# A streaming encoder layer: pool weights folded into the output projection, norm roots by DRAM, more column groups, slots of a multiple of 256 bytes, and products of two contraction blocks in turn

## The chip, the cores and the metric

The kernel runs on 1 core of one Trainium2 chip. The metric is the device time of the program in microseconds, the median of several runs. TensorE (PE in the profile) does matrix products, VectorE is DVE, ScalarE is ACT, GpSimd is POOL; SyncE (SP) issues most DMAs. PSUM has eight banks of 128 x 512 float32, SBUF holds the tiles.

## The reference

One layer of a hybrid encoder, applied to 2048 prompt frames and to 32 frames of a running stream (the sample), with model width 1024. Everything is float32.

```python
def layer(x, pool_hist, n_valid, S0, ...):
    h = rmsnorm(x, g_pre_mix)
    z = h @ w_in                                  # 1024 x 2560: u, q, f, i, g of 512 columns each
    u, zq, zf, zi, zg = jnp.split(z, [...], axis=-1)
    u_ext = concat([pool_hist, u], axis=1)
    y_pool = pool_mix(u_ext, n_valid, w_pool, pool_scale)
    ...                                           # q, gate f, key, log f from zq, zf
    S1, o = hgrn_run(S0, q, kin, zi, logf)        # gated recurrence, 4 heads x 128
    y_hg = rmsnorm(o, g_hg_norm) * silu(zg)
    y_mix = concat([y_pool, y_hg], axis=-1) @ w_out
    x = x + rmsnorm(y_mix, g_post_mix)
    h2 = rmsnorm(x, g_pre_ffn)
    f = (silu(h2 @ w_gate) * (h2 @ w_up)) @ w_down   # 1024 x 2816 and back
    x = x + rmsnorm(f, g_post_ffn)
    return x, u_ext[:, -15:], S1

def pool_mix(u_ext, n_valid, w_pool, pool_scale):
    for g, w in enumerate((2, 4, 8, 16)):         # 4 groups of 128 channels
        d_g = (trailing sum of w frames) / min(t + 1 + n_valid, w) - u_g
    y = einsum('blgc,gcd->blgd', d, w_pool)       # one 128 x 128 map for each group
    return y * pool_scale
```

## The kernel before

**Precision.** Every large product is made of three TensorE products in float32r: each operand is split into a high part (ScalarE copies it to float32r) and a low part (VectorE subtracts), and high x high, high x low and low x high are summed in a PSUM bank. A product of 128 x 128 stationary and 128 x 512 moving elements is the unit; the program has 8,232 of them. Small work (pool maps, the recurrence's blocks, transposes, the sample's frames) is done in plain float32, where one product is two passes in the trace.

**Stages.** The prompt is worked in two halves of 1024 frames, A (`S.B` False) and B (`S.B` True), B with the 32 sample frames. For each half, in TensorE's order: the values (`first_values` or `values`: the i columns, frames stationary), four heads (`head_products`: columns f, q and g, weights stationary, activations `hT` moving, in banks `mmb`), four pool groups 3, 2, 1, 0 (`pool_products`), the output projection (`project`, banks `ops`), then gate and up (`gate_up`, banks `gx`, `gy`, `gz`, `gw`, with seven products in place of eight for each pair of blocks). At the end `down` makes the second feed-forward product for all frames (banks `dx`, `dy`, `dz`).

**What runs between.** The recurrence of a head (`hgrn`), the pool windows, norms and statistics are written as generators. A `Task` holds one; `poll()`, called after every three products, advances those whose time has come on a clock `Pace.t` that adds an assumed time for each TensorE instruction. So TensorE's order is fixed when the program is written; the orders of the other engines and of SP's DMAs come from the framework's scheduler. `finish()` makes all that is left of a task. `take()`, `ahead()` and `raws()` load and split weight blocks some steps ahead of their use.

**The recurrence's blocks.** `group` makes 32 x 16 or 32 x 32 blocks of scores for each 32 frames, with the output in the PSUM partitions 32j to 32j+31 of the bank `gb`: four column groups. The level-5 blocks go to partitions 0 and 64 (two column groups), the 64 x 64 blocks `lv` to partitions 0 to 63 (one).

**The pool stage.** `pool_window` makes the windowed means on VectorE directly behind a group's products. `pool_mix`, a task, multiplies by `w_pool` on TensorE (bank `pps`, full float32, 128 x 512, two for a group and half), scales and splits the result into `S.y[g]`, and in B transposes the last 15 frames of each group out (`nps`).

**The norm at B's start.** `later_stats` sums the squares of B's frames while A runs. `front_norm` spreads the roots over the partitions: POOL makes diagonal matrices `dg`, and TensorE multiplies them by ones (bank `rb`). The sample's frames are scaled and transposed by TensorE (`stps`). `late_constants` loads `w_pool` and transposes the pool cache (`cps`).

**Memory.** Tiles live in slots: 39 of `TMAX` = 1056 float32 (4,224 bytes, 16.5 times 256), and `NT` = 22 of 512 float32 (2,048 bytes). Slots stand one behind the other, so every second slot of the first kind starts 128 bytes past a multiple of 256.

Of the kernel before, what the change touches and what calls it, by code (L numbers as in the profile page):

```python
# [29 lines left out]
NT = 22  # L30
# [4 lines left out]
TMAX = HALF + NS  # L35
CHUNK = 128
# [41 lines left out]
def body(tc, ins, outs, cst):  # L78
    nc = tc.nc
    ctx = ExitStack()  # L80
    with ctx:
# [7 lines left out]

        def ztile(name, shape=None, dt=F32):  # L90
            return UP.tile(shape or [P, TMAX], dt, tag="u", name=name)

        def xtile(name, shape=None):
            return UP.tile(shape or [P, TMAX], F32R, tag="u", name=name)

# [45 lines left out]
        wpool = CP.tile([P, 4, P], F32, name="wpool")  # L141
        hist = CP.tile([P, 4, 16], F32, name="hist")
        shist = CP.tile([P, 4, 16], F32, name="shist")
# [9 lines left out]
        def late_constants():  # L153
            nc.sync.dma_start(out=wpool, in_=ins["w_pool"][0].rearrange("g c d -> c g d"))
            cachet = ztile("cachet", [HIST, 512])
            nc.sync.dma_start(out=cachet, in_=ins["cache_pool"][0, 0])
            cps = axbank("cps")
            for g in range(4):
                nc.tensor.transpose(cps[:, 16 * g:16 * g + HIST], cachet[:, g * P:(g + 1) * P], ident[0:HIST, 0:HIST])
            nc.vector.tensor_copy(shist[:, :, 0:HIST], cps[:, 0:64].rearrange("p (g t) -> p g t", g=4)[:, :, 0:HIST])  # L160
# [113 lines left out]

        def gemm_cols(w, act, n0, n1, ps):
            _, hi, lo = w
            n = n1 - n0
            cnt = 3 * len(act)
            i = 0
            for k, (ah, al) in enumerate(act):  # L280
                wh, wl = (x[k // 4][:, (k % 4) * P:(k % 4 + 1) * P] for x in (hi, lo))
                for a, b in ((wh, ah), (wh, al), (wl, ah)):
                    mm(ps[:, 0:n], a, b[:, n0:n1], i == 0, i == cnt - 1, rcost(n))
                    i += 1
                poll()
# [151 lines left out]
        def later_stats(S):  # L437

            st = S.st
            for i in range(NCH):  # L440
# [6 lines left out]
                yield 20000.0  # L447
            ev = st[:, 0:16].rearrange("p (i c) -> p i c", c=2)
# [3 lines left out]
            S.rs = [[st[:, 24 + 4 * tg + i:25 + 4 * tg + i] for i in range(4)] for tg in range(2)]  # L452

        def scaled_channels(S, tg):
            rb = axbank("rb")
            for i in range(4):
                mm(rb[:, i * P:(i + 1) * P], ones, S.dg[tg][:, i], True, True, 112.0)
# [17 lines left out]
        def front_norm(S, tg):  # L475
            if tg == 0:
                S.hsr = SP.tile([P, KD, NS], F32, tag="hs", name="hsr", bufs=1)
                S.ysr = SP.tile([P, KD, NS], F32, tag="ysr", name="ysr", bufs=1)
            channel_tiles(S, tg)
            S.dg[tg] = t2("dg", [P, 4, P])  # L480
            for i in range(4):
                nc.gpsimd.tensor_scalar(S.dg[tg][:, i], ident, S.rs[tg][i], None, ALU.mult)
            if tg == 1:
                xq = ztile("xts", [NS, D])
                nc.sync.dma_start(out=xq, in_=x_s)
# [3 lines left out]
            if tg == 1:  # L489
                st = new_stat()  # L490
                sumsq(xq, NS, st[0:NS, 0:1])
                nc.vector.tensor_scalar(xq, xq, rstd_of(st, NS), None, ALU.mult)
            yield from scaled_channels(S, tg)
            if tg == 1:
                sample_to_channels(xq, g_pre, S.hsr)


        def front_loads(S):
# [111 lines left out]
        def values(S, tg):  # L610
# [4 lines left out]
            for k in range(0, KD, 2):  # L615
# [5 lines left out]
                for kk in range(2):  # L621
                    ah, al = S.hT[k + kk]
                    for i in range(4):
                        value_products(pss, i, ah, al, (tg * 4 + i) * P, hi[kk], lo[kk], k + kk == 0, k + kk == KD - 1)
                        poll()
# [1080 lines left out]
```

## Time and profile before

| | |
|---|---|
| median of 3 runs | 2145.66 us (2145.22 to 2146.64) |
| the profiled execution | 2145.8 us, of which the span is 2144.0 |
| granted TensorE clock | 0.998 of full speed |
| TensorE | 99% busy, 13,176 passes |
| VectorE, ScalarE, GpSimd | 67%, 38%, 13% busy |
| DMA | 316.19 MB moved, 147 GB/s on average |

A span is the time from the first to the last instruction. A row of the profile names a line, an engine, an operation, and the tile written and the tiles read. TensorE's line is nearly always L180, the helper `mm`, so rows are told apart by their tiles. A product's length in the trace, some 0.39 us, has its drain in it; what counts is the time from one product's start to the next's. "x434" counts instructions, and idle time stands behind a bar with what ended it.

### The profile page before, as it was taken

The page shows a single profiled execution, that of the slowest core. Times are in us where ns is not written, and L with a number is a line of the kernel's source. Part 1 is how long each engine was busy: PE and PEld are TensorE (multiplying, and loading weights), DVE is VectorE, ACT ScalarE, POOL GpSimd, SP SyncE. Part 2 cuts the span into 40 slices and gives each one's busy share as a digit, 9 for nine tenths or more (in the row PEclk, how much of TensorE's full clock was granted, in tenths as well). Part 3 has the DMA queues.
Part 4 walks back from the last instruction along what each step waited for, and adds up shares of the span by engine and source line. Part 5 has one row for each costly group of instructions (what it writes and reads, how often), then busy time and mean ns, then how long its engine had stood idle before and what let it go on. Part 6 is the DMA issues. An engine that isn't in the chain of part 4 may idle for free.

```text
span 2144.0 us, 34134 instructions
## 1 busy us (share of the span) xinstructions
PE 2124.1 (99%) x13176; PEld 1702.8 (79%) x13176; DVE 1431.6 (67%) x2330; ACT 822.0 (38%) x1605; POOL 281.6 (13%) x382
## 2 busy tenths in 40 slices
PE   9999999999999999999999999999999999999998
PEld 8788778888888887788867778888888777877876
DVE  6655665787776778355574697767667756466487
ACT  6434335544444445233323664444444521011032
POOL 1223301100000010122320220000000211110134
PEclk9999999999999999999999999999999999999999
DMA  8121134445545559011004624544445796776778
GB/s 305 50 70 56 35 128 157 128 123 167 157 144 156 148 162 286 27 44 34 25 23 149 189 85 131 156 143 143 144 143 145 234 323 197 224 222 189 223 214 217
DMA packets 388783, 316.19 MB, mean 147 GB/s; under 512 B 16007, under 2 KB 318335, under 8 KB 388622
## 3 DMA queue, kind: packets, MB, share of 16 engines
q1 hardware_dynamic: 386174, 306.11, 46.5%
q0 software_dynamic: 2016, 7.34, 1.8%
q8 instruction: 104, 1.70, 0.3%
q14 instruction: 57, 0.47, 0.1%
q10 hardware_dynamic: 432, 0.57, 0.1%
HBM read 215.60 MB, written 98.37 MB: 146 GB/s over the span
## 4 chain that ended last, share of the span: by engine, by line
PE 82%; DVE 4%; ACT 1%; issue 1%; POOL 1%; DMA 1%; DVEq 0%; POOLq 0%; SPq 0%; ACTq 0%
PE gx L180 21%; PE gy L180 11%; PE dx L180 10%; PE mmb L180 10%; PE ops L180 9%; PE dy L180 5%; PE gz L180 4%; PE dz L180 3%; PE vps L180 2%; PE gw L180 1%; PE gsps L180 1%; PE gb L180 1%; DVE acc L1493 1%; PE ups L180 1%; PE pps L180 1%
## 5 line engine op out<-in xcount | busy, mean ns | idle before, releaser
L180 PE MATMUL gx<-fhi,wf 128*128 128x512 f32 x1376 | 449.1, 395 | 0.0
L180 PEld LDWEIGHTS gx<-fhi,wf 128*128 128x128 f32 x1376 | 258.3, 188 | 61.4 <-issue 2.2
L180 PE MATMUL gx<-flo,wf 128*128 128x512 f32 x688 | 270.0, 392 | 0.0
L180 PE MATMUL gy<-fhi,wf 128*128 128x512 f32 x704 | 233.0, 393 | 0.1
L180 PE MATMUL mmb<-hThi,whi 128*128 128x512 f32 x512 | 217.6, 425 | 0.0
L180 PE MATMUL dx<-dhi,hst 128*128 128x512 f32 x640 | 213.4, 394 | 0.5 <-DVE acc L1493 0.4
L180 PE MATMUL mmb<-hThi,wlo 128*128 128x512 f32 x512 | 201.7, 394 | 0.0
L180 PE MATMUL mmb<-hTlo,whi 128*128 128x512 f32 x512 | 201.5, 394 | 0.0
L1493 DVE TENSOR_TENSOR acc<-dx,acc 128x512 f32<-128x512 f32 x168 | 115.2, 689 | 75.9 <-PE dx L180 75.2
L1217 DVE TENSOR_TENSOR wf<-s,wf 128x512 fp32r<-128x512 f32 x176 | 120.1, 689 | 62.2 <-ACT wf L1212 59.6
L180 PEld LDWEIGHTS gy<-fhi,wf 128*128 128x128 f32 x704 | 132.2, 188 | 31.2 <-DVE c L1315 0.5
L180 PEld LDWEIGHTS gx<-flo,wf 128*128 128x128 f32 x688 | 129.4, 188 | 28.3
L1212 ACT CAST wf<-s 128x512 fp32r<-128x512 f32 x176 | 108.3, 621 | 101.0 <-PE gy L180 30.3
L180 PEld LDWEIGHTS dx<-dhi,hst 128*128 128x128 f32 x640 | 120.1, 188 | 32.2 <-issue 3.4
L180 PE MATMUL gy<-flo,wf 128*128 128x512 f32 x352 | 138.2, 393 | 0.0
L180 PE MATMUL dx<-dlo,hst 128*128 128x512 f32 x320 | 125.5, 392 | 0.0
L1217 DVE TENSOR_TENSOR wf<-wraw,wf 128x512 fp32r<-128x512 f32 x132 | 89.8, 688 | 44.2 <-ACT wf L1212 44.1
L180 PEld LDWEIGHTS mmb<-hThi,whi 128*128 128x128 f32 x512 | 96.6, 189 | 24.4 <-issue 5.4
L180 PEld LDWEIGHTS mmb<-hThi,wlo 128*128 128x128 f32 x512 | 96.4, 188 | 22.3
L180 PE MATMUL dy<-dhi,hst 128*128 128x512 f32 x320 | 112.9, 393 | 1.0 <-DVE acc L1493 1.0
L1212 ACT CAST wf<-wraw 128x512 fp32r<-128x512 f32 x132 | 80.9, 621 | 83.5 <-PE gx L180 38.3
L180 PEld LDWEIGHTS mmb<-hTlo,whi 128*128 128x128 f32 x512 | 96.8, 189 | 18.7 <-issue 2.4
(332 smaller groups left out, 4093.2 us busy)
## 6 DMA issues: line engine op xcount, KB each, us to landing
hst<-hdFalse SPq DMA_DIRECT2D x140, 256.0 KB, 3.0
hst<-hdTrue SPq DMA_DIRECT2D x140, 256.0 KB, 3.1
wraw<-in_w_gate_dram SPq DMA_DIRECT2D x50, 512.0 KB, 4.2
wraw<-in_w_up_dram SPq DMA_DIRECT2D x50, 512.0 KB, 4.1
hdFalse<-hhi SPq DMA_DIRECT2D x77, 256.0 KB, 2.3
hdFalse<-hlo SPq DMA_DIRECT2D x77, 256.0 KB, 2.4
hdTrue<-hhi SPq DMA_DIRECT2D x77, 256.0 KB, 2.6
hdTrue<-hlo SPq DMA_DIRECT2D x77, 256.0 KB, 2.6
```

What stands on the lines that cost most here:

```text
L180: nc.tensor.matmul(out, l, r, start=start, stop=stop, skip_group_check=more)
L1212: nc.scalar.copy(wf[:, 0], getattr(M, src) if isinstance(src, str) else src)
L1217: nc.vector.tensor_tensor(wf[:, 1], getattr(M, src) if isinstance(src, str) else src, wf[:, 0].bitcast(F32), ALU.subtract)
L1493: nc.vector.tensor_tensor(dst, ps, dst, ALU.add)
```

## The change

1. **Slots.** `SLOT` = 1024 + 64 float32 (4,352 bytes, 17 times 256) takes the place of 1056; `NT` is 21. `wpool` and `shist` are gone from the constants.

```diff
-NT = 22
+NT = 21
+SLOT = HALF + 64
-            return UP.tile(shape or [P, TMAX], dt, tag="u", name=name)
+            return UP.tile(shape or [P, SLOT], dt, tag="u", name=name)
```

2. **Products in turn.** `in_turn` takes the three products of two contraction blocks alternately, so that no product has an operand of the one before it. It is used in `gemm_cols`, `values`, `project`, and the `product` of `gate_up` and `down` (where the group has one pair, the three are only put into another order). `first_values` keeps its order.

```diff
+        def in_turn(trios):
+            for a, b in ((0, 2), (0, 3), (1, 2)) if len(trios) > 1 else ((0, 2), (1, 2), (0, 3)):
+                for t in trios:
+                    yield t[a], t[b]
...
-                for kk in range(4):
-                    bh, bl = (x[:, (kk % 2) * 512:(kk % 2) * 512 + 512] for x in F[kk // 2])
-                    wh, wl = wf[:, 0, kk * P:(kk + 1) * P], wf[:, 1, kk * P:(kk + 1) * P]
-                    for n, (a, b) in enumerate(((wh, bh), (wh, bl), (wl, bh))):
-                        mm(ps, a, b, start and kk == 0 and n == 0, kk == 3 and n == 2, rcost(512), not start)
-                    poll()
+                for k in (0, 2):
+                    trios = [(*(wf[:, i, kk * P:(kk + 1) * P] for i in range(2)),
+                              *(x[:, (kk % 2) * 512:(kk % 2) * 512 + 512] for x in F[kk // 2])) for kk in (k, k + 1)]
+                    for n, (a, b) in enumerate(in_turn(trios)):
+                        mm(ps, a, b, start and k == 0 and n == 0, k == 2 and n == 5, rcost(512), not start)
+                        if n % 3 == 2:
+                            poll()
```

3. **Pool weights folded.** A task in half A makes `mixed` = w_pool x scale x the first 512 rows of w_out, writes it to DRAM, and the projections load those rows from there. The windowed mean goes to the projection without a map between; `pool_mix` and its products are gone. The windows are a task now, with VectorE's steps 1300 ns apart.

```diff
+        def mixed_weights():
+            wt = t2("wpt", [P, 4, P])
+            nc.sync.dma_start(out=wt, in_=ins["w_pool_t"].rearrange("g d c -> d g c"))
...
+            load(*todo[0])
+            yield 6000.0
             for g in range(4):
+                nc.scalar.activation(wt[:, g], wt[:, g], AF.Copy, scale=p_scale[:, g:g + 1])
+            for n, (g, dh) in enumerate(todo):
+                if n + 1 < len(todo):
+                    load(*todo[n + 1])
+                ps = axbank("wmp")
+                mm(ps, wt[:, g], rows.pop((g, dh)), True, True, 858.0)
+                out = t2("wmo")
+                nc.scalar.copy(out, ps)
+                nc.sync.dma_start(out=mixed[g * P:(g + 1) * P, dh * 512:dh * 512 + 512], in_=out)
+                yield 4000.0
...
-                        want(lambda ki=ki, dh=dh: raw_rows2(w_out, KORDER[ki], dh * 512))
+                        want(lambda ki=ki, dh=dh: raw_rows2(mixed if KORDER[ki] < 4 else w_out, KORDER[ki], dh * 512))
...
-                ps = axbank("pps")
-                mm(ps, wpool[:, g, :], d_t[:, sbk * 512:(sbk + 1) * 512], True, True, 858.0)
...
+            put_y(S, g, slice(0, HALF), d)
```

4. **Roots by DRAM, inputs in channels.** `later_stats` also sums the sample's squares and writes the 1,056 roots to DRAM; B's `front_norm` loads them broadcast over the partitions in place of `dg` and `rb`. The sample's frames and the pool cache come transposed as inputs, so `stps` of the first norm and `cps` are gone. The eight `nps` transposes are one.

```diff
+            nc.gpsimd.tensor_tensor(st[0:NS, 35:36], st[0:NS, 34:35], nhalf[0:NS, 0:1], ALU.pow)
+            nc.sync.dma_start(out=roots[0, 0:HALF].rearrange("(i p) -> p i", p=P), in_=st[:, 24:32])
+            nc.sync.dma_start(out=roots[0, HALF:TMAX].rearrange("(p i) -> p i", i=1), in_=st[0:NS, 35:36])
...
+            S.rb[tg] = t2("rb")
+            nc.sync.dma_start(out=S.rb[tg], in_=roots[0:1, tg * 512:tg * 512 + 512].broadcast_to([P, 512]))
-            for i in range(4):
-                nc.gpsimd.tensor_scalar(S.dg[tg][:, i], ident, S.rs[tg][i], None, ALU.mult)
```

5. **Column groups.** The level-5 blocks go to four column groups, `lv` to two; ScalarE copies them out in twice as many pieces.

```diff
-                    c0 = c * P + 32 * j
-                    mm(gb[c // 4][32 * j:32 * j + 32, o:o + 32], k_t[:, c0:c0 + 32], qa[:, c0 + 32:c0 + 64], True, True, 55.0)
+                    c0, q = c * P + 32 * j, 32 * (j + c % 2)
+                    mm(gb[c // 4][q:q + 32, o:o + 32], k_t[:, c0:c0 + 32], qa[:, c0 + 32:c0 + 64], True, True, 55.0)
...
-                mm(lv[0:64, c * 64:c * 64 + 64], k_t[:, c * P:c * P + 64], qa[:, c * P + 64:c * P + 128], True, True, 112.0)
+                q, o = c % 2 * 64, c // 2 * 64
+                mm(lv[q:q + 64, o:o + 64], k_t[:, c * P:c * P + 64], qa[:, c * P + 64:c * P + 128], True, True, 112.0)
```

How this moves instructions shows in the orders of the built programs. First TensorE, in a pool group of half A, before; `hThi_320` and `hTlo_321` are the parts of one contraction block of the activations, `_322` and `_323` of the next, `whi` and `wlo` the weights:

```order
L180 MATMUL mmb<-hThi_324,whi 128x512
L180 MATMUL mmb<-hTlo_325,whi 128x512
L180 MATMUL mmb<-hThi_324,wlo 128x512
L180 MATMUL pps<-sb,wpool 128x512
L180 MATMUL mmb<-hThi_326,whi 128x512
L180 MATMUL mmb<-hTlo_327,whi 128x512
L180 MATMUL mmb<-hThi_326,wlo 128x512
```

The same place now:

```order
L200 MATMUL mmb<-hThi_324,whi 128x512
L200 MATMUL mmb<-hThi_326,whi 128x512
L200 MATMUL mmb<-hTlo_325,whi 128x512
L200 MATMUL mmb<-hTlo_327,whi 128x512
L200 MATMUL mmb<-hThi_324,wlo 128x512
L200 MATMUL mmb<-hThi_326,wlo 128x512
```

The pool product is gone, and what were three products of one block and three of the next alternate. Second, TensorE at the start of head 0 in half A, where nothing stood between the products before:

```order
L200 MATMUL mmb<-hThi_316,whi 128x512
L200 MATMUL mmb<-hThi_318,whi 128x512
L200 MATMUL mmb<-hTlo_317,whi 128x512
L200 MATMUL wmp<-wmr,wpt 128x512
L200 MATMUL mmb<-hTlo_319,whi 128x512
L200 MATMUL mmb<-hThi_316,wlo 128x512
```

That is the first of the eight products that fold the weights (`wmr`: rows of w_out; `wpt`: the scaled pool weights); the other seven follow through this head. Third, SP's queue at the same time, before (`wraw` are head weights, `xtl` B's frames for the statistics):

```order
L424 DMA xt<-in_x_prompt_dram 128x1024 x4
L154 DMA wpool<-in_w_pool_dram 128x4x128
L897 DMA S_8778<-in_state_hgrn_dram 128x128
L231 DMA wraw<-in_w_in_dram 128x8x128 x3
L156 DMA cachet<-in_cache_pool_dram 15x512
L231 DMA wraw<-in_w_in_dram 128x8x128 x3
L444 DMA xtl<-in_x_prompt_dram 128x512 x2
```

And now:

```order
L452 DMA xt<-in_x_prompt_dram 128x1024 x4
L526 DMA hsr<-x_sample_channels 128x8x32
L945 DMA S_8821<-in_state_hgrn_dram 128x128
L971 DMA es<-cache_channels 128x15 x2
L251 DMA wraw<-in_w_in_dram 128x8x128 x5
L159 DMA wpt<-w_pool_t 128x4x128
L165 DMA wmr<-in_w_out_dram 128x512 x2
L251 DMA wraw<-in_w_in_dram 128x8x128
L178 DMA mixed<-wmo 128x512
L165 DMA wmr<-in_w_out_dram 128x512
L178 DMA mixed<-wmo 128x512
```

The transfers for folding stand between the heads' weights, and each store of `mixed` waits in the queue for its product.

More of the change, by code (lines that the diff above doesn't have):

```diff
@@ L916, in pool_products @@
         def pool_products(S, g):
+            if S.B and g == 3:
+                S.tail = small("kds", [P, 2, 4, HIST], bufs=2)
             e_t = ztile("e_t")
@@ L959, in pool_mix @@
[L959 to L970 removed]
+                nc.gpsimd.tensor_copy(S.tail[:, 0, g], e_t[:, HALF:HALF + HIST])
@@ L971, in pool_mix @@
+                nc.gpsimd.tensor_copy(S.tail[:, 1, g], es[:, NS:NS + HIST])
+            yield from window(e_t, HALF, (sa, sb), d, not S.B)
+            yield 1300.0
+            S.y[g] = (ztile("yhi", dt=F32R), ztile("ylo", dt=F32R))
+            put_y(S, g, slice(0, HALF), d)
             if S.B:
                 yield 0.0
-                ps = axbank("pps")
-                mm(ps[:, 0:NS], wpool[:, g, :], S.ds[g][:, 0:NS], True, True, 218.0)
-                nc.vector.tensor_scalar(S.ysr[:, g, :], ps[:, 0:NS], p_scale[:, g:g + 1], None, ALU.mult)
```

198 lines of the change are left out of this document (104 added, 94 removed).

## The prediction

> **What bounds the kernel now.** I read the page's busy times first, then TensorE's waits, then a stretch without breaks, then single products.
>
> ```profile
> span 2144.0 us, 34134 instructions
> PE 2124.1 (99%) x13176; PEld 1702.8 (79%) x13176; DVE 1431.6 (67%) x2330; ACT 822.0 (38%) x1605; POOL 281.6 (13%) x382
> ```
>
> TensorE (PE) is busy 99% of the span, while the next engine, DVE, has a third of its time free. A busy PE may still be slower than it could be, so its waits come next: who waited for whom, with the total in us, the times and the longest.
>
> ```profile
> PE gb L180 <- ACT f_t L789: 2.5, 1, 2.5
> PE gb L180 <- POOL k_t L757: 1.8, 1, 1.8
> ```
>
> These are the two longest; all of PE's waits come to about 10 us, half a per cent. So the kernel lasts as long as PE's own stream, and two things shorten it: fewer or cheaper instructions there, or a closer sequence of the 8,232 split products (128x512, float32r) that make up nearly all of it. How close they stand shows where nothing else runs: the table by windows (us, then busy time and count of PE, PEld, DVE, ACT, POOL, granted clock, DMA share, GB/s).
>
> ```profile
> 600.00:700.00 100.00, 100.00 (x434) 81.31 (x434) 69.62 (x110) 46.02 (x82) 0.00 (x0) 1.00 0.50 146
> ```
>
> 434 products in 100 us are 230.4 ns each, at a granted clock of 1.00. Over the whole trace 7,768 of the 8,231 steps from one product's start to the next's are shorter than 300 ns; their mean is 230.9.
>
> **The change, part by part. Aligned slots and neighbours.** The trace has exactly as many split products as the program, so each row can be set beside the addresses that its operands have in the built program. In it 4,462 of the 8,232 pairs have a moving and a stationary operand whose addresses differ by an odd multiple of 128 bytes; in the changed program none has. Pairs of neighbours with one stationary operand fall from 2,740 to 60. What the first of these costs shows in the timeline (start and length in us, engine, line, operation). A stretch of TensorE where all operands are a multiple of 256 bytes apart:
>
> ```profile
> 1261.30 0.39 PE L180 MATMUL gw<-flo,wf 128*128 128x512 f32 x1
> ...
> 1264.02 0.39 PE L180 MATMUL gw<-flo,wf 128*128 128x512 f32 x1
> ```
>
> And one where a product's moving and stationary operand never are:
>
> ```profile
> 1460.46 0.63 PE L180 MATMUL gx<-fhi,wf 128*128 128x512 f32 x2
> 1460.92 0.40 PE L180 MATMUL gx<-flo,wf 128*128 128x512 f32 x1
> ...
> 1462.79 0.40 PE L180 MATMUL gy<-fhi,wf 128*128 128x512 f32 x1
> ```
>
> In the first, 12 steps take 2.72 us, 226.7 ns each; in the second, 10 steps take 2.33 us, 233 ns. The whole trace says the same: of 2,358 groups of three products with one stationary high part, 501 wholly aligned ones stand at 229.5 ns and 706 wholly misaligned ones at 232.0, and all 39 aligned groups behind nine or more aligned products stand at 226.7. Misalignment thus costs some 6 ns at its worst and is carried on over about eight products. With every operand aligned I take 226.7 ns, and 230.4 from the window as before: 8,231 x 3.7 ns = **30.5 us less**. (From the mean of 230.9 it would be 34.5; the 4 us between I leave to the products behind some 240 breaks, which have to fall into step again.) The bounds: 11 us if short aligned groups (229.5) are all there is, 34.5 at full effect.
>
> The new order by itself I cost at nothing. In the locked stretch the step between two neighbours with one stationary operand (fhi to flo) is as long as the two steps without: 227, 227 and 226 ns. In aligned groups that aren't locked the shared step is 230.5 against 229.0, so up to 1.5 ns on a third of the steps, 4 us, is the gain if the lock doesn't come; and 224 ns, the shortest step that occurs often, bounds it below: 8,231 x 2.7 = 22 us more. That it loses is bounded by the step with a shared moving operand, 232 ns, which the change also makes rarer.
>
> A rule of the Trainium skill speaks against all this part. TensorE: Matmul & The Clock Gate (Part 2, step 1, LDWEIGHTS) says that PE has two independent read ports, one for the streaming operand and one for weights, so that loading the next weights takes no bandwidth from the running product. By it neither addresses nor neighbours matter and this term is 0, not 30.5 us. The two stretches above speak against it: one kind of product, one clock, 226.7 and 233 ns.
>
> **PE work removed and added.** A product of the pool stage (full fp32, two passes):
>
> ```profile
> 281.26 0.40 PE L180 MATMUL mmb<-hThi,wlo 128*128 128x512 f32 x1
> 281.49 1.02 PE L180 MATMUL pps<-sb,wpool 128*128 128x512 f32 x2
> 282.58 0.39 PE L180 MATMUL mmb<-hTlo,whi 128*128 128x512 f32 x1
> ...
> L180 PE MATMUL pps<-sa,wpool 128*128 128x512 f32 x16 | 8.3, 599 | 0.2 <-DVE ylo L968 0.2
> L180 PE MATMUL pps<-sb,wpool 128*128 128x512 f32 x16 | 8.3, 598 | 0.0
> L180 PE MATMUL pps<-es,wpool 128*128 128x32 f32 x8 | 1.3, 246 | 0.0
> ```
>
> From 281.26 to 282.58 there are two split products and one pps: 1.32 - 2 x 0.231 = 0.86 us. The group rows count passes, so 16 pps go: 13.7 us; the four for the sample tokens (es) have 1.3 us of busy time, of which I take 0.9. The folding adds eight products of the same shape (wmp), 6.9 us. All stand on PE, which has no free time, so all count.
>
> Blocks of 32 and 64 rows put into two, or twice as many, column groups:
>
> ```profile
> 98.25 0.39 PE L180 MATMUL mmb<-hThi,wlo 128*128 128x512 f32 x1
> 98.56 0.70 PE L180 MATMUL gb<-qa,k_t 128*32 128x32 f32 x32
> 99.53 0.40 PE L180 MATMUL mmb<-hTlo,whi 128*128 128x512 f32 x1
> ...
> 91.99 0.73 PE L180 MATMUL gb<-qa,k_t 128*32 128x16 f32 x64
> 92.64 0.50 PE L180 MATMUL mmb<-hThi,whi 128*128 128x512 f32 x1
> ...
> 103.22 0.40 PE L180 MATMUL mmb<-hThi,wlo 128*128 128x512 f32 x1
> 103.55 1.15 PE L180 MATMUL lv<-qa,k_t 128*64 128x64 f32 x16
> 104.96 0.40 PE L180 MATMUL mmb<-hTlo,whi 128*128 128x512 f32 x1
> ```
>
> The level-5 block (gb, 32 passes in two column groups) takes 1.28 - 0.46 = 0.82 us, lv (16 passes in one) 1.74 - 0.46 = 1.28. In four groups 64 passes take 0.65 us, 10 ns each, where the 32 take 20. So twice the groups can save at most half of a block's own time (0.70 us of busy time less the 0.20 of its last pass, and 1.15 less 0.22); the change of shape at both ends stays. I take that half, 0.25 and 0.46 us, eight times each: 2.0 + 3.7 us (between 0 and 5.7). ScalarE pays with 48 more small copies, beside PE: it is busy 38%.
>
> The norm's roots by DRAM, the caches by DMA:
>
> ```profile
> 795.18 0.40 PE L180 MATMUL gz<-fhi,wf 128*128 128x512 f32 x1
> 795.42 1.05 PE L180 MATMUL rb<-dg,ones 128*128 128x128 f32 x8
> 796.54 0.39 PE L180 MATMUL gy<-flo,wf 128*128 128x512 f32 x1
> ...
> L979 PE MATMUL nps<-cons,es 128*15 128x128 f32 x4 | 1.1, 275 | 0.0
> L979 PE MATMUL nps<-cons,e_t 128*15 128x128 f32 x4 | 1.1, 274 | 0.4 <-DVE on L838 0.4
> L369 PE MATMUL stps<-cons,xts 32*128 32x32 f32 x8 | 0.7, 225 | 0.0
> L159 PE MATMUL cps<-cons,cachet 15*128 15x15 f32 x4 | 0.4, 213 | 0.0
> ```
>
> Two rb blocks go at 1.36 - 0.46 = 0.90 us: 1.8. Of the small transposes seven of eight nps, stps of the first norm and cps go: 3.2 us of busy time at most, 2.2 taken, since their drains overlap. Sum of this part: 13.7 + 0.9 - 6.9 + 2.0 + 3.7 + 1.8 + 2.2 = **17.4 us less** (between 10 and 19).
>
> **What the change makes wait.** Four places, and I cost each at nothing.
> The wmp products stand in head 0's stream and wait for a 256 KB row block and the scaled weights; behind them stands all of head 0. Each load is issued one step (4,000 ns of the planner's time) before its use:
>
> ```profile
> hst<-hdFalse SPq DMA_DIRECT2D x140, 256.0 KB, 3.0
> SPq L1473 <- PE dx L180: 130.4, 129, 3.1
> 1700.00:1800.00 100.00, 99.58 (x433) 76.92 (x432) 55.65 (x78) 24.64 (x39) 9.57 (x4) 1.00 0.88 282
> ```
>
> A block of that size lands 3.0 us after its issue. Late by 1 us at each of eight, it would cost 8 us.
> The sample rows' root (three POOL operations on a sum from ScalarE) stands on POOL between head 3's last k_t merges; PE's lv waits for these, and SP's loads for the projection stand behind the store of the roots. Priced by the longest such wait above, 1.8 us, up to three times: 5 us.
> One tile less for transfers (21 for 22) only shortens the lead of the hidden tiles: SP waits there for PE to free one (second row), not for bandwidth, though the DMA share of 0.88 (third row) leaves little.
> In projection and values both blocks of a pair are needed from the first product on, 12 products (2.8 us) earlier than now for the second; the splits run two pairs ahead.
>
> The sum, against the profiled execution's 2145.8 us (span 2144.0 and 1.8 around it; the median of the runs is 2145.66): 2145.8 - 30.5 - 17.4 = **2098 us**.
>
> **Rivals.** (a) Addresses and neighbours don't set the rate: 2145.8 - 17.4 = 2128. Against it stand the two stretches. It is what the quoted rule gives. (b) The lock at 226.7 isn't kept, since operands change in another order, and the rate is that of short aligned groups, 229.5: 2145.8 - 11 - 17.4 = 2117. For it: only 39 groups show the lock. (c) Neighbours without a common operand go closer than 226.7: down to 224, 2076, or less. No long stretch of such neighbours exists in the trace. The same page of the Trainium skill (Part 1, "Wait — 56ns, not 53.3ns?") gives 215.7 ns from start to start for 512 columns; by it, as an estimate, the time would be about 2005. (d) The new waits show: wmp late and lv behind the roots, 8 + 5 us: 2111. (e) Slower: the second block's weights aren't split in time. There are 40 such pairs (32 in the projections, 8 in B's values); a pair late by all of 2.8 us costs 111 us in sum. It decides from 48 / 40 = 1.2 us per pair on; at 1.8 us it is 2145.8 - 48 + 72 = 2170. Against it: today PE's waits for whi or wlo don't appear among its waits. (f) That the change doesn't do what it says: it does, by the counts of addresses and neighbours above.
>
> **How the numbers follow.** The forecast 0.54; (a) 0.11, (b) 0.13, (c) 0.08, (d) 0.10, (e) 0.04. The range takes in (a), (b), (d) and the near part of (c): 2078 to 2128; outside are (e) and the far part of (c), with tails of the rest. What a measurement here can tell from no change is 0.2%, 4.3 us: faster 0.94, same 0.02, slower 0.04.
>
> **What would show it.** In the windows without breaks some 441 products in 100 us, not 434; steps of 226 to 227 ns for long stretches. No pps, 16 passes wmp of 0.86 us a pair, no wait of wmp for a DMA; lv with about 0.6 us less from product to product, no rb in B. Above 2115 us either the steps stand at 229 ns and more, which refutes the lock, or PE's waits have grown beyond 10 us, which says that PE no longer sets the end.

## The result, and the profile after

| | before | after |
|---|---|---|
| median of 4 runs each, on one chip | 2145.73 us (2145.22 to 2146.64) | 2110.61 us (2108.03 to 2111.26) |
| ratio, 95% interval | | 0.9835 [0.9821, 0.9850] |
| span of the profiled execution | 2144.0 us | 2108.8 us |
| mean step of the split products, all steps under 300 ns | 230.86 ns (7,768) | 227.38 ns (7,782) |
| idle time between PE's instructions, in sum | 11.4 us | 18.9 us |

The change saves 35 us; 2098 were forecast, 13 us less than came out. First the page of after:

```profile
span 2108.8 us, 34100 instructions
PE 2081.5 (99%) x13117; PEld 1690.4 (80%) x13117; DVE 1423.5 (68%) x2302; ACT 831.6 (39%) x1659; POOL 283.4 (13%) x387
```

PE is still busy 99%, so the bound is the same engine. The table by windows shows that the products stand closer (columns as in the prediction):

```profile
305.00:355.00 50.00, 50.00 (x222) 41.41 (x221) 24.57 (x36) 21.25 (x45) 9.38 (x18) 1.00 0.34 123
600.00:700.00 100.00, 100.00 (x443) 82.79 (x442) 70.80 (x112) 46.97 (x84) 0.00 (x0) 1.00 0.52 150
```

443 products in the 100 us that held 434, at the same clock. Over the whole trace 8,231 x (230.86 - 227.38) ns = 28.6 us. The 200-odd runs of small work between split products, without the waits in them, take 16.6 us less (214.6 us before, 198.0 after: the time from the last split product ahead to the second one behind, less two mean steps each). That makes 45.2 us, but the span fell by 35.2. So 10 us were lost again, 7.5 of them as idle time (18.9 - 11.4). PE's waits, listed by who ended them, say where:

```profile
PE mmb L200 <- issue: 5.6, 1, 5.6
PE gb L200 <- issue: 3.5, 2, 3.1
PE vps L200 <- ACT va L670: 2.3, 1, 2.3
```

None of the three stands in the profile of before. The first two are called "issue": PE stood still, and nothing that the profile records released it. The timeline of PE around them (a number in brackets is the idle time ahead of the row):

```profile
235.43 0.39 PE L200 MATMUL mmb<-hTlo,whi 128*128 128x512 f32 x1
236.16 0.44 PE L200 MATMUL gb<-qa,k_t 128*32 128x16 f32 x31 [0.35 <-issue]
239.72 0.80 PE L200 MATMUL gb<-qa,k_t 128*32 128x16 f32 x33 [3.12 <-issue]
240.44 0.80 PE L200 MATMUL mmb<-hTlo,whi 128*128 128x512 f32 x1
241.04 1.05 PE L200 MATMUL mmb<-hThi,wlo 128*128 128x512 f32 x2
247.72 1.22 PE L200 MATMUL mmb<-hThi,whi 128*128 128x512 f32 x2 [5.63 <-issue]
248.74 1.05 PE L200 MATMUL mmb<-hTlo,whi 128*128 128x512 f32 x2
249.59 1.05 PE L200 MATMUL mmb<-hThi,wlo 128*128 128x512 f32 x2
250.58 0.75 PE L200 MATMUL gb<-qa,k_t 128*32 128x16 f32 x64
```

A run of 64 gb passes breaks in the middle, which its data can hardly cause, since the operands are the same two tiles throughout. Behind the waits a pair of products takes 1.05 us where 0.62 is usual (steps of 427 ns for 227): behind the first long wait PE ran at half the granted clock, until 250.6 us. The waits called issue are 9.1 us in all, and eight slow steps and two slow gb runs cost some 2.8 more: 12 us. (Before had waits of its own that after hasn't, so the net loss is smaller.) What else is there? SP's queue just ahead, and the DMAs of the window 225 to 256 us (tile, count, KB each, us from issue to landing):

```profile
229.30 0.38 SPq L489 DMA_DIRECT2D roots<-st_b  x1
229.73 0.58 SPq L251 DMA_DIRECT2D wraw<-in_w_in_dram  x1
230.40 0.54 SPq L258 DMA_DIRECT2D wrow<-in_w_out_dram  x1
```

```profile
DMA packets 2498, 1.22 MB, mean 39 GB/s; under 512 B 1152, under 2 KB 2176, under 8 KB 2496
...
q8 instruction: 2, 0.03, 0.4%
...
wraw<-in_w_in_dram SPq DMA_DIRECT2D x1, 512.0 KB, 14.2
wrow<-in_w_out_dram SPq DMA_DIRECT2D x1, 512.0 KB, 15.1
```

The store of the roots (1,024 elements of 4 bytes) was issued at 229.3 us, and the two loads behind it landed after 14 and 15 us. On the page the fifty loads of that size and form (`wraw<-in_w_gate_dram`) have a median of 4.2. The experiments had to settle two things, then: whether the addresses or the new order made the 28.6 us, and whether this store lost the 12.

### The profile page after: what moved, and what is told of

It is laid out like the page before. It is cut to its first block, busy times and chain, and to the rows that moved or that the text cites. A ratio compares the mean times of both kernels' runs of the same rounds, so it can differ in the third digit from the quotient of the medians.

```text
span 2108.8 us, 34100 instructions
## 1 busy us (share of the span) xinstructions
PE 2081.5 (99%) x13117; PEld 1690.4 (80%) x13117; DVE 1423.5 (68%) x2302; ACT 831.6 (39%) x1659; POOL 283.4 (13%) x387
## 4 chain that ended last, share of the span: by engine, by line
PE 88%; DVE 6%; issue 2%; DMA 1%; ACT 1%; POOL 1%; SPq 0%; DVEq 0%; POOLq 0%; ACTq 0%
PE gx L200 21%; PE mmb L200 15%; PE gy L200 10%; PE dx L200 10%; PE ops L200 10%; PE gz L200 5%; PE dy L200 5%; PE vps L200 3%; PE dz L200 2%; PE gb L200 1%; DVE acc L1533 1%; PE gw L200 1%; PE gsps L200 1%; PE ups L200 1%; PE tps L343 1%
## 5 line engine op out<-in xcount | busy, mean ns | idle before, releaser
L200 PE MATMUL gx<-fhi,wf 128*128 128x512 f32 x1376 | 387.3, 391 | 0.0
L200 PE MATMUL gx<-flo,wf 128*128 128x512 f32 x688 | 213.0, 390 | 0.0
L200 PE MATMUL gy<-fhi,wf 128*128 128x512 f32 x704 | 201.8, 390 | 0.1
L200 PE MATMUL dx<-dhi,hst 128*128 128x512 f32 x640 | 185.3, 391 | 0.8 <-DVE acc L1533 0.6
L200 PE MATMUL mmb<-hTlo,whi 128*128 128x512 f32 x512 | 177.4, 407 | 0.0
L200 PE MATMUL mmb<-hThi,whi 128*128 128x512 f32 x512 | 166.4, 406 | 5.6 <-issue 5.6
L200 PE MATMUL mmb<-hThi,wlo 128*128 128x512 f32 x512 | 159.9, 394 | 0.0
L1472 ACT CAST dhi<-t 128x1024 fp32r<-128x1024 f32 x20 | 20.6, 1052 | 232.2 <-DVE dlo L1473 163.7
L200 PE MATMUL gy<-flo,wf 128*128 128x512 f32 x352 | 108.7, 389 | 0.0
L200 PE MATMUL dy<-dhi,hst 128*128 128x512 f32 x320 | 98.6, 389 | 1.1 <-DVE acc L1533 1.1
```

The costliest lines, as they stand in the source:

```text
L200: nc.tensor.matmul(out, l, r, start=start, stop=stop, skip_group_check=more)
L1472: nc.scalar.copy(hi, src)
```

## Experiments: addresses or order

Five kernels come from the changed one, and a sixth from the one before. The order undone:

```diff
-            for a, b in ((0, 2), (0, 3), (1, 2)) if len(trios) > 1 else ((0, 2), (1, 2), (0, 3)):
-                for t in trios:
-                    yield t[a], t[b]
+            for t in trios:
+                for a, b in ((0, 2), (0, 3), (1, 2)):
+                    yield t[a], t[b]
```

> The changed kernel with one thing undone: the three products of one contraction block again follow one another, so that 2,740 neighbours share a stationary operand (the changed kernel has 60); all 8,232 big products stay aligned (0 at an odd multiple of 128 B). Theory (the addresses made the gain, the order nothing): 2111 us, within 4, and dense steps of 227.4 ns as after the change. Rival (the order made the gain): steps back near the 230.9 ns of before, so 8,231 x 3.5 ns = 29 us more, 2139. Between them (both are needed: a row of three on one stationary operand stays at the 229.5 ns that 501 aligned ones had in the trace of before): 8,231 x 2.1 ns = 17 us more, 2128.

The slot undone; every engine's instructions and their order stay the same:

```diff
-SLOT = HALF + 64
+SLOT = TMAX
```

> The changed kernel with one number undone: a slot holds 1,056 elements (4,224 B) again and not 1,088 (4,352 B). Every engine's instructions stay the same, in the same order; only addresses differ: 4,497 of the 8,232 big products have their operands an odd multiple of 128 B apart (0 after the change, 4,462 before it). Theory (addresses): steps back to 230.9 ns, 8,231 x 3.5 ns = 29 us more, 2139. Rival (the order made the gain): 2111, within 4.

Both undone:

> The changed kernel with both undone, the order of the products and the slot (4,177 misaligned products, 2,740 neighbours with a shared stationary operand, near the 4,462 and 2,740 of before). Theory (addresses alone): as the slot undone alone, 2139, within 4. Rival (order alone): as the order undone alone. If each does part, the two effects add up to this one's, near 2139; if either is enough to lose the gain, all three are near 2139.

A gap of 128 bytes between the pool of the large slots (activations, split rows of the values and of the gate) and that of the small ones (split weights of the projections):

```diff
         UP = ctx.enter_context(tc.tile_pool(name="up", bufs=NU))
+        GP = ctx.enter_context(tc.tile_pool(name="gp", bufs=1))
         TP = ctx.enter_context(tc.tile_pool(name="tp", bufs=NT))
...
+        gap = GP.tile([P, 32], F32, name="gap")
+        nc.gpsimd.memset(gap, 0.0)
...
-            return small("st", [P, 4], bufs=20)
+            return small("st", [P, 4], bufs=16)
```

> The changed kernel with 128 unused bytes between the two pools that hold the operands: products with one operand in each pool become misaligned, those with both in one pool do not. That is all 2,304 products of the head and pool projections and of the output projection (mmb, ops) and 1,680 of the 1,848 of the down projection (dx, dy, dz); none of the 3,696 of gate and up (gx, gy, gz, gw) and of the 384 of the second half's values (vps). Nothing else is changed but that small statistics tiles have 16 buffers and not 20. Theory (the two operands' addresses against each other): the three stages lose 3 to 5 ns a step, 3,984 x 4 ns = 16 us more, 2127 (2123 to 2131), and gx, gy stay at 226.6 to 227.4 ns. Rival (only the order, or the size of the slot): 2111, every stage as after the change.

And the same gap with 16 elements, 64 bytes:

> As the kernel with 128 unused bytes between the operands' two pools, with 64 B: the same 3,984 products (mmb, ops, and 1,680 of dx, dy, dz) have operands 64 or 192 B apart by the address modulo 256, the rest 0. If any offset but a multiple of 256 B costs the same: the three stages at 232.3 to 232.8 ns, 2127. If it is only the 128-B bit that counts: half of the run of a row crosses it and half doesn't, between 227 and 232.5 ns, 2112 to 2125. If offsets under 128 B are free: every stage as after the change, 2111. No theory of mine prefers one of these; the run is there to find the size of the step.

Last, the kernel before with the slot alone:

```diff
-NT = 22
+NT = 19
+SLOT = HALF + 64
...
-            return UP.tile(shape or [P, TMAX], dt, tag="u", name=name)
+            return UP.tile(shape or [P, SLOT], dt, tag="u", name=name)
...
-            return UP.tile(shape or [P, TMAX], F32R, tag="u", name=name)
+            return UP.tile(shape or [P, SLOT], F32R, tag="u", name=name)
```

> The kernel before with one part of the change alone, the slot of 4,352 B: all 8,232 products aligned (4,462 were not), and the old order with its 2,740 shared neighbours; 19 tiles for transfers in place of 22 make the room. Theory (addresses alone): steps of 227.4 ns for 230.9, 8,231 x 3.5 ns = 29 us less than before, 2117 (2114 to 2120). Rival (the alignment helps only with the new order around it, or three tiles fewer cost a wait): 229.5 ns or some us of waits for DMA, 2125 to 2140.

"Misaligned" counts the products whose two operands don't lie a multiple of 256 bytes apart, "shared" the neighbours with one stationary operand. Steps are means of all steps under 300 ns within a stage, in ns; "heads" are the head and pool projections (mmb), "gate" is gx, "output" is ops, "down" is dx.

| kernel | misaligned | shared | heads | gate | output | down | median us | ratio to before |
|---|---|---|---|---|---|---|---|---|
| before | 4,462 | 2,740 | 230.95 | 230.76 | 231.92 | 230.66 | 2145.7 | |
| after | 0 | 60 | 229.14 | 227.02 | 227.11 | 227.30 | 2110.6 | 0.9835 [0.9821, 0.9850] |
| order undone | 0 | 2,740 | 229.12 | 227.04 | 227.10 | 227.27 | 2109.6 | 0.9834 [0.9819, 0.9849] |
| slot undone | 4,497 | 60 | 230.92 | 231.21 | 232.35 | 231.81 | 2137.1 | 0.9962 [0.9947, 0.9977] |
| both undone | 4,177 | 2,740 | 231.02 | 230.28 | 232.18 | 230.63 | 2133.6 | 0.9944 [0.9929, 0.9959] |
| 128 bytes between | 3,984 | 60 | 232.52 | 227.04 | 232.33 | 232.80 | 2127.2 | 0.9915 [0.9899, 0.9932] |
| 64 bytes between | 3,984 | 60 | 233.28 | 226.98 | 229.04 | 233.01 | 2127.0 | 0.9911 [0.9894, 0.9927] |
| before, slot alone | 0 | 2,740 | 228.96 | 227.00 | 227.19 | 227.26 | 2120.3 | 0.9879 [0.9863, 0.9896] |

With aligned slots the order does nothing: undone, it moves no stage of the table by more than 0.03 ns. Nor does a shared stationary operand save a weight load: the profile counts 13,117 of them (PEld) with either order. The slot does all of it. The gate window of the kernel with the order undone, then with the slot undone, to be held against the 443 products of after and the 434 of before:

```profile
600.00:700.00 100.00, 100.00 (x443) 82.82 (x442) 70.78 (x112) 47.09 (x85) 0.00 (x0) 1.00 0.52 152
```

```profile
600.00:700.00 100.00, 100.00 (x434) 81.16 (x433) 70.42 (x112) 46.39 (x82) 0.00 (x0) 1.00 0.53 150
```

Undone alone the slot costs 26.5 us; added alone to the kernel before it gives 25.0 of the 29 expected, and 2120.3 us lies just above the range set out for it. (In its trace the steps have the full 227.3 ns; PE waits 2.5 us more than before, 13.9 us in all.) The kernel with only the slot undone lost less than its steps say (231.40 ns on average, 8,231 x 4.0 = 33 us): PE's idle time is 4.3 us shorter there than in after (14.6 for 18.9), 2.3 of it the third wait of the list above, at vps, which is gone. The rest of the difference is not accounted for.

One run missed: with both undone 2139 was expected and 2133.6 came. So without aligned slots the old order is 3.5 us faster than the new one. It also has 320 fewer misaligned products, and which of the two made the difference no run shows.

The gap between the pools is the sharpest of these runs, because it splits one execution into stages that it touches and stages that it doesn't. The windows of the kernel with 128 bytes, to be held against after's two above:

```profile
305.00:355.00 50.00, 50.00 (x217) 40.55 (x216) 23.34 (x37) 19.19 (x39) 7.47 (x16) 1.00 0.34 123
600.00:700.00 100.00, 100.00 (x443) 82.81 (x442) 71.43 (x113) 46.42 (x82) 0.00 (x0) 1.00 0.54 154
```

In the output projection (first row) there are 217 products for 222; in gate and up (second row), whose operands lie in one pool, 443 as after the change. DVE, ACT and the DMAs work about as much as there. It cost 16.6 us; 16 were expected. The same rows with 64 bytes:

```profile
305.00:355.00 50.00, 50.00 (x220) 41.04 (x219) 24.47 (x37) 18.63 (x40) 7.46 (x16) 1.00 0.37 133
600.00:700.00 100.00, 100.00 (x443) 82.79 (x442) 71.49 (x113) 46.84 (x84) 0.00 (x0) 1.00 0.53 153
```

So 64 bytes cost as well, and not in every stage alike: in the output projection the moving operand lies 64 bytes further than the stationary one (modulo 256), and the step is 229.0 ns; in heads and down projection it lies 192 further, and the step is 233. This can also be read in another way. Every product that a gap touches has one operand in the pool that moved: the moving one in the output projection, the stationary one in heads and down. So these two runs don't tell whether the distance between the operands counts or the place of one of them. The prediction sorted the trace of before by the distance, which speaks for the first; no run separates the two. None of the three cases that I had set out for this run fits as put: "any offset costs the same" gives the time, but not the output projection's 229.0.

## Experiments: the store of the roots

The roots as rows: TensorE turns the 128x9 block of roots, and DRAM gets eight rows of 512 bytes and one of 128.

```diff
...
+            yield 40000.0
+            ps = axbank("rtp")
+            nc.tensor.transpose(ps[0:9, 0:P], st[:, 24:33], ident)
+            tick(107)
+            rt = small("S0", [9, P], bufs=2)
+            nc.vector.tensor_copy(rt, ps[0:9, 0:P])
...
-            nc.sync.dma_start(out=roots[0, 0:HALF].rearrange("(i p) -> p i", p=P), in_=st[:, 24:32])
+            nc.sync.dma_start(out=roots[0, 0:HALF].rearrange("(i p) -> i p", p=P), in_=rt[0:8])
...
```

> The changed kernel with the roots of the second half written to DRAM as nine rows: TensorE turns the 128x9 block of roots (some 40 us of products later, so that it waits for nothing), DVE copies it to 9x128, and two stores write rows of 512 and 128 B in place of 1,024 and 32 elements of 4 B. What is read back is the same. Theory (the 4-byte store holds up the DMA rings behind it, the loads and PE's own instructions, so that PE stands 3.1 + 5.6 us at 237 to 248 us and then runs at half the granted clock for some us): both waits called issue go, and the slow stretch with them, 11 to 13 us less than the change, 2098 to 2100. Rival (the instructions come late for another reason, the store is only near by): both waits stay, 2111. Second rival (the waits go, but PE then waits for the next late thing there, the merges of that head or the sample root): one wait of 2 to 5 us in their place, 2103 to 2107.

Measured: 2097.5 us (2096.1 to 2100.0), ratio 0.9778 [0.9763, 0.9792]. PE's longest waits there:

```profile
PE gb L200 <- DVE qa L809: 1.9, 5, 0.7
PE dx L200 <- DVE acc L1540: 1.1, 3, 0.5
```

Both waits called issue are gone, and so is the stretch at half the clock. The window of that head in after, then in this kernel:

```profile
200.00:300.00 100.00, 90.58 (x804) 74.19 (x803) 61.03 (x103) 38.81 (x106) 27.03 (x39) 0.95 0.20 56
```

```profile
200.00:300.00 100.00, 99.45 (x855) 82.52 (x855) 69.96 (x116) 44.14 (x113) 26.60 (x37) 1.00 0.29 97
```

51 more passes fit into the same 100 us. The opposite test, the 4-byte store issued twice:

```diff
             nc.sync.dma_start(out=roots[0, 0:HALF].rearrange("(i p) -> p i", p=P), in_=st[:, 24:32])
+            nc.sync.dma_start(out=spare[0, 0:HALF].rearrange("(i p) -> p i", p=P), in_=st[:, 24:32])
```

> The changed kernel with the store of 1,024 roots of 4 B issued a second time, right behind the first, to a place in DRAM that nothing reads. Theory (the 4-byte store holds up the DMA rings): twice the hold-up, so the waits called issue near 237 to 260 us grow from 8.7 us to 16 to 20 us in all, 2119 to 2123. Rival (it is not the store): 2111, waits as after the change.

Measured: 2118.6 us (2117.6 to 2119.2), 8 us more, a little under what was expected. Waits, and landings of the loads behind:

```profile
PE gb L201 <- issue: 11.9, 5, 8.4
PE mmb L201 <- issue: 3.3, 1, 3.3
```

```profile
wraw<-in_w_in_dram SPq DMA_DIRECT2D x1, 512.0 KB, 23.3
wrow<-in_w_out_dram SPq DMA_DIRECT2D x1, 512.0 KB, 23.9
```

One store more delays the next load from 14.2 to 23.3 us, 9.1 us for 1,024 elements, and PE's waits called issue grow from 9.1 to 15.2 us (5.6 + 3.5 and 11.9 + 3.3).

But the kernel with rows stores them elsewhere: its small product waits its turn in PE's order, and SP issues the store at 396 us, no longer in head 3. Two more kernels were to separate the form from the place. The 4-byte form at the late place (`mm` with the identity keeps the block as 128x9):

> The kernel that stores the roots as rows, with the form of the store alone turned back: at the same place in every queue (SP issues it at 396 us there, where loads for gate and up run, no longer at 229 us in head 3), TensorE's small product keeps the block as 128x9 and the stores write 1,024 and 32 elements of 4 B again. Theory (it is the form of the store, wherever it stands): the loads and PE's instructions behind it come 10 us and more late once more, PE waits some 9 us near 400 to 420 us, 2107 to 2111. Rival (the place: only in the heads, with their many short instructions, does PE need new instructions so soon; between the long rows of gate and up what it holds lasts over the hold-up): the loads behind the store still land late, but PE shows no wait, 2098 within 3.

And rows, brought forward (3,000 and 5,000 for the waiting times of 100,000 and 40,000 in the planner's clock):

> The kernel that stores the roots as rows, with the store brought forward into head 3, some five loads behind the place that the 4-byte store has in the changed kernel; behind it stand loads of the output weights. TensorE's small product comes with it. With the runs so far (4-byte store early 2111, late 2100, rows late 2097.5) this is the fourth corner. Theory (form: 9 rows hold up nothing, wherever they stand): no wait of PE called issue, 2097 to 2101. Rival (place: any store to DRAM at that point holds up the loads and instructions behind it): waits called issue of several us, 2104 to 2111.

| | early: 4 B at 229 us, rows at 258 us | at 396 us |
|---|---|---|
| 1,024 elements of 4 B | 2110.6 (2108.0 to 2111.3) | 2100.4 (2097.3 to 2101.9) |
| 8 rows of 512 B | 2098.0 (2097.8 to 2098.4) | 2097.5 (2096.1 to 2100.0) |

The place is shown: the same 4-byte store costs 10 us less at 396 us than in head 3, so the theory that the form counts wherever it stands (2107 to 2111) falls. What the form is worth is shown less well. At 396 us it makes 2.9 us, and the ranges overlap. The early rows don't stand where the 4-byte store stood: they wait for PE's small product and are issued 28 us later, when the last run of 64 gb passes (at 239 us in that kernel) is long over. So no run has rows in front of those runs. The late 4-byte store is just as slow by itself:

```profile
roots<-S SPq DMA_DIRECT2D x1, 4.0 KB, 8.9
```

8.9 us for 4 KB; yet PE shows no wait. SP has no further load to issue until 428 us, and only one packet of instructions falls into this time; it takes 3.4 us, with rows 0.95.

```profile
395.00:405.00 10.00, 10.00 (x57) 8.42 (x56) 9.38 (x17) 7.17 (x16) 0.00 (x0) 1.00 0.19 38
405.00:415.00 10.00, 10.00 (x45) 8.28 (x45) 10.00 (x13) 6.01 (x10) 0.00 (x0) 1.00 0.00 0
```

The early rows hold up nothing; a load of the output weights, issued 0.7 us behind them, lands after 3.8:

```profile
257.51 0.32 SPq L496 DMA_DIRECT2D roots<-S  x1
257.88 0.22 SPq L497 DMA_DIRECT2D roots<-S  x1
258.20 5.36 SPq L258 DMA_DIRECT2D wrow<-mixed  x2
```

```profile
wrow<-mixed SPq DMA_DIRECT2D x1, 512.0 KB, 3.8
```

What was it that PE waited for in after? The queue that brings instructions (q8) shows no packet between 223.8 and 245.2 us, and PE goes on from the second wait 2.5 us behind the latter. The other kernels with the 4-byte store in head 3 do the same: 20.7 to 21.3 us without a packet, 29.0 with the store issued twice, and in all eight PE goes on 2.2 to 2.6 us behind the packet that ends it. The four that store late or in rows have the next packet after 6.4 to 7.9 us, and PE makes neither stop. That the second wait is for instructions is therefore more than a guess, though no run tried it by itself. A run of 64 small blocks takes 0.65 us of PE's time, in which there are some three long products, so in a head instructions are used up some twenty times faster for a while. That may be why the place matters; that loads stand right behind the store in head 3, and none at 396 us, may be another reason.

The first wait is not explained by this: it ended at 239.7 us without a packet. In the kernel with the order undone it is put down to POOL, and there DVE and POOL stand still as well, until 239.5 and 239.6 us, for a cause that the profile doesn't name:

```profile
PE gb L200 <- POOL k_t L801: 5.0, 1, 5.0
```

What the runs do show is that the 4-byte store in that place makes both stops: moved away it makes none, and doubled it makes them 6.1 us longer.

## Experiments: the small work

Column groups undone, level 5 and lv:

```diff
-                o = 384 + c % 4 // 2 * 32
+                o = 384 + c % 4 * 32
...
-                    c0, q = c * P + 32 * j, 32 * (j + c % 2)
+                    c0, q = c * P + 32 * j, 32 * j
...
-                q, o = c % 2 * 64, c // 2 * 64
+                q, o = 0, c * 64
                 mm(lv[q:q + 64, o:o + 64], k_t[:, c * P:c * P + 64], qa[:, c * P + 64:c * P + 128], True, True, 112.0)
...
```

> The changed kernel with one part undone: the small products of the sixth and seventh level (gb of level 5, and lv) stand in one column group again, as before, and ACT copies them out with the fewer, larger copies of before. Theory (the two column groups made the runs shorter by what the traces show, lv 1.281 to 0.806 us in 8 runs, level 5 0.819 to 0.580 us in 8 runs): 8 x 0.475 + 8 x 0.239 = 5.7 us more than the change, 2116. Rival (ACT's eight additional small copies in each head pay for it, or the time goes to waits): within 2 us of the change, 2109 to 2113.

Measured: 2114.6 us (2113.2 to 2118.0), 4.0 more. The lv block in after, then here:

```profile
107.45 0.39 PE L200 MATMUL mmb<-hTlo,whi 128*128 128x512 f32 x1
107.77 0.69 PE L200 MATMUL lv<-qa,k_t 128*64 128x64 f32 x16
108.38 0.50 PE L200 MATMUL mmb<-hTlo,whi 128*128 128x512 f32 x1
```

```profile
107.85 0.39 PE L200 MATMUL mmb<-hTlo,whi 128*128 128x512 f32 x1
108.17 1.15 PE L200 MATMUL lv<-qa,k_t 128*64 128x64 f32 x16
109.24 0.50 PE L200 MATMUL mmb<-hTlo,whi 128*128 128x512 f32 x1
```

From product to product 0.93 us, and 1.39 without the groups: 0.46 us, eight times, is 3.7 us, and the eight runs of level 5 add 1.9. Some of that came back, as the wait at vps shrank from 2.3 to 0.6 us.

The folding left out, in the kernel with rows (its output projection reads the rows of w_out as they are, so the pool maps and the pool scale are missing from its result):

> The kernel that stores the roots as rows, and leaves out the folding: the eight products of the pool weights with the output weights, their loads and stores and the pool scale aren't computed, and the output weights are read as they are. Theory (every product on PE counts in full, there and in the terms of the sum): 8 x 0.86 us = 6.9 us and the wait of 0.6 us less, 2090 within 2. Rival (part of it was hidden in waits that PE has anyway): 2094 to 2098.

Measured: 2091.8 us (2091.3 to 2092.3), 5.7 less than the 2097.5 with it. The 6.9 us of PE's work went, and a wait of 1.8 us that the kernel with the folding doesn't have came:

```profile
PE gb L200 <- POOL k_t L808: 1.8, 1, 1.8
```

## Why the prediction came out as it did

**The bound.** PE's stream set the end, before and after. Of work put onto PE or taken off, 4.0 of 5.6 us and 5.7 of 6.9 showed in the time; the rest went into waits on other engines. In these two runs an engine that is 99% busy passed on most of a saving, not all of it. The forecast's range, 2078 to 2128 us, holds the 2110.6 measured; the 2098 in its middle was missed by 12.6 us. The steps gave 1.9 us less than taken, the small work 0.8, and some 10 were lost to waits and a slow clock that had been put at nothing.

**Aligned slots, 30.5 us.** Right in cause, and nearly in size: 28.6 by the steps, 25.0 and 26.5 in the two runs that change the slot alone. What was mis-sized is the step. 226.7 ns is reached, in every stage: from the twelfth product behind a break on, 365 steps of the heads have a mean of 226.67 and 5,823 others 226.68. But the first eleven behind a break stand at 230.1 (907 in the heads, 687 elsewhere), and the heads' small work breaks their rows so often that 71% of their steps are among the first eleven. That makes 227.4 overall. The prediction had set 4 us aside for the breaks; 5.9 went (34.5 at full effect, 28.6 measured).

**The new order, nothing.** Right: 2109.6 against 2110.6. Rival (b), that the lock needs the old neighbours, and rival (c), that neighbours with nothing in common go closer, both fall with it. Rival (a) falls with the slot. So does the rule that the prediction quoted against itself. By the Trainium skill, TensorE: Matmul & The Clock Gate (Part 2, step 1, LDWEIGHTS), loading the next weights takes no read bandwidth from the running product. By that 128 bytes between two pools should cost nothing; here they cost 16.6 us, and the measurement decides. Why they cost it no run shows.

**PE's small work, 17.4 us.** The trace shows 16.6 less, and in the kernel with rows 17.5 (214.6 and 197.1). lv lost 0.46 us a block, as taken.

**What the change makes wait.** Here the prediction failed. It named the right place, SP's loads behind the store of the roots in head 3, but what it priced was the wait of that store for the sample's root, 5 us at worst, and it took nothing. That wait came (SP stands 12.8 us at the first store of roots and 22.2 at the second), and none of PE's waits names it. The transfer itself it never priced: 1,056 writes of 4 bytes, which cost some 12 us with the slow clock behind them. A row of before for a store of that form was not there, and that should have been a term with bounds. On this point the Trainium skill had the hint: DMA: Bandwidth & Descriptors (Specifications) says that under 512 B a transfer is a read, a change and a write. The trace agrees as far as the price goes (8.9 us for 4 KB in elements of 4 B, against 4.2 for 512 KB in the loads); no run shows the read. With the roots in rows, and late, the time is 2097.5 us. That this meets the 2098 of the forecast has some luck in it: the steps gave some 2 us less than taken, and PE's idle time, 8.9 us, is 2.5 below that of before.

The other three waits stayed small: wmp waited 0.6 us for its rows, once; neither the 21 tiles nor the second block of a pair appears among PE's waits, so rival (e) had no part in it. Rival (d) gave 2111, which is the number measured, but for 8 us at wmp and 5 at lv. By its parts it was wrong.

**Left open.** The wait of 2.3 us at vps, behind evictions that stand on ACT after casts for the next frames. In that stretch DVE, which makes what is cast, is busy without a break:

```profile
826.00:838.00 12.00, 9.71 (x43) 7.69 (x42) 12.00 (x19) 7.08 (x12) 0.00 (x0) 0.99 0.70 206
```

In the other runs of the changed kernel with aligned slots it lasts between 0.4 and 2.3 us, without a rule that I can name. No run was made for it.

**The better version.** The change with the roots in rows beats both kernels: 2097.5 us, 0.9778 of before against 0.9835.

## What to carry to other kernels

Check where the two operands of a product lie before reordering products: here one number, the slot's size in bytes, was worth 25 to 26 us and the order nothing, and a gap between two pools tests it in one run, stage by stage. Count a store by its elements, not its bytes; turn a column into rows before it goes to DRAM, and keep it away from runs of small blocks (the place alone was worth 10 us here). When PE waits for "issue" and nothing released it, look at what the DMA queues did in the 20 us before, the one that brings instructions too.

## What the runs showed of the hardware

- Float32r products of 128x128 by 128x512 follow one another in 226.7 ns when the moving and the stationary operand lie a multiple of 256 bytes apart. With the moving one 64 bytes further (modulo 256) the mean step of the output projection is 229.0 ns; with 128 the stages stand at 232.3 to 232.8, with 192 at 233.0 to 233.3.
- After a break such a row needs some eleven products, at 230.1 ns on average, until it stands at 226.7; misaligned rows never get there (heads with 128 bytes between: 232.35 ns in the first eleven, 232.96 behind them).
- A store of 1,024 elements of 4 B took 8.9 us, and a second one behind it delayed the next load by 9.1. Behind eight rows of 512 B with the same content, at 258 us, a load of 512 KB landed after 3.8.
- With the 4-byte store in a head the instruction queue brought no packet for some 21 us, 29 with two such stores; without it the next packet came after 6.4 to 7.9 us.
- With PE's two stops of 3.1 and 5.6 us the granted clock went to 0.50, from 240.4 to 250.6 us: the mean from 236 to 251 us is 0.66.
